# Differential attention heads written out in a fixed order of VectorE, ScalarE and GpSimd

## The chip, the cores and the metric

The kernel runs on one core of one Trainium2 chip. A core has a matrix engine (TensorE, "PE" in the profile; its weight loads are "PEld"), VectorE ("DVE"), ScalarE ("ACT"), GpSimd ("POOL") and SyncE ("SP"), which issues most of the loads. The engines run side by side, each works off its own list of instructions in order, and they wait for one another through semaphores. The metric is the device time of one execution in microseconds (us): the median over runs, before against after.

## The reference

One block of a streaming encoder over 512 tokens (T) of width 1024 (D), float32, one layer. It adds three terms to the residual stream x:

```python
h = rms_norm(x, attn_norm_g)
z = h @ w_in                                   # MLA latents | diff q | diff k | diff v
y_mla  = mla_group(...)                        # 8 heads, 64 wide
y_diff = diff_group(...)                       # 4 heads, 128 wide
x = x + concat([y_mla, y_diff]) @ w_out
x = x + conv_ffn(rms_norm(x, ffn_norm_g), ...) # 1024 -> 2816 -> 1024, causal conv, silu
x = x + sigmoid(rms_norm(x, ple_norm_g) @ w_ple_gate) * (p @ w_ple_proj)
```

The part that matters here is the differential group. Each of its 4 heads has two query and key halves (m = 0, 1; 64 wide), one value (128 wide), and a bias by relative position:

```python
logits = q[m] @ k[m].T * scale + bias          # masked block-causally
probs  = softmax(logits)
attn   = probs[0] - lam * probs[1]
o      = rms_norm(attn @ v, out_g) * (1 - lam_init)
```

## The kernel before

Everything is kept as tiles of 128 partitions. A float32 matrix product is made of three products of rounded halves: an operand is split into a high half (a cast to fp32r on ScalarE) and a low half (the rest, a subtraction on VectorE), and `mm3` (L152) issues high x high, high x low and low x high. So every operand that comes out of a transpose costs one ScalarE and one VectorE instruction before TensorE can use it (`split`, L180): TensorE takes the high half of an activation first and its low half one matmul later. Weights are loaded by SyncE into a ring of three buffers (`load_raw`, L138) and split in the same way, 128x1024 at a time (`load_w`, L143; ScalarE L148, VectorE L149).

The kernel goes through input projection, MLA heads (8 heads x 4 query tiles), differential heads (4 heads h x 4 query tiles t, list `dslots`, L709), the output projection, the feed-forward part, and the per-layer gate. TensorE's order is that of the program text throughout (`manual_schedule`, L98). VectorE, ScalarE and GpSimd follow the program text only inside regions; outside them a planner orders their instructions by its own estimate of readiness. Before the change, there is no region from the fifth step of the MLA heads to the end of the differential heads; the planner may move work forward there, and a few places are tied to an earlier instruction by `issue_after`. The feed-forward region begins at L847.

The differential loop (L767 to L782) has 16 steps i = 4h + t. In step i it issues the logits of step i + 2 (`diff_logits`, L662), some "fill" units of the output projection, the transposes of the probabilities of step i (`probs_T`, L533, with a copy out of PSUM on ScalarE, L541), and the product with the values of step i - 1 (`diff_pv`, L685). For each m, `diff_logits` issues three TensorE products, VectorE's sum with the bias that also gives the row maximum (L675), ScalarE's exponential with its row sum (L676); then VectorE combines both m (L680 to L682). Keys and queries of the next head are transposed and split in step t = 0 (`diff_T`, L654). After the last value product of a head, ScalarE squares the output and copies it out, VectorE reduces the squares, GpSimd raises to the power -0.5, and VectorE scales (L693 to L707). The scaled output is transposed and split in step t = 2 of the next head (`y_split`, L613).

A fill unit is six matmuls of 128x512: `wo_units` (L638) makes the output projection for a block b of 128 output columns; the first 16 units (kq = 0, two per block) use the MLA outputs, the last four (kq = 1) the outputs of differential heads 0 and 1. A finished block is added to the residual on VectorE (`add_x`, L630). `FILL_DIFF` (L63) says how many units each step takes. After the loop come products of what is still missing (`early`, L801), in which the output of head 2 is needed first and that of head 3 from the transposes at L805 on; then the feed-forward part's first weights.

PSUM has eight banks: "lg" 3 for logits, "tp" 2 for transposes, "acc" 2 for the output projection, "ob" 1 for the head's output. A transpose into "tp" waits until the bank's last reader is done.

Of the kernel before, what the change touches and what calls it, by code (L numbers as in the profile page):

```python
# [62 lines left out]
FILL_DIFF = ((2, 1, 1, 1), (1, 1, 2, 1), (1, 2, 2, 1), (1, 1, 2, 2))  # L63
# [26 lines left out]
def _f32(ap):  # L90
    return ap.bitcast(F32)
# [3 lines left out]
def hybrid_block(ctx: ExitStack, tc: tile.TileContext, a: dict, out: bass.AP):  # L95
# [537 lines left out]
    wo2 = {}  # L633

    def wo_w(kq, dq):
        return load_w(a["w_out"][kq, dq], 1024, f"o{kq}{dq}")

    def wo_units(kq, dqs, nk):  # L638

        for dq in dqs:  # L640
            w = wo_w(kq, dq)
            if kq:
                wo2[dq] = w
            for b in (2 * dq, 2 * dq + 1):
                ps = bank("acc", f"o{kq}{b}")
                for k in range(0, nk, 2):
                    mm3(ps, wo_blocks(4 * kq + k, 4 * kq + k + 2, b, w), k == 0, k == nk - 2)
                    if k == nk - 2:
                        add_x(b, ps)
                    yield  # L650
# [3 lines left out]
    def diff_T(h, c):  # L654
        ps = bank("tp" if h else "acc", f"d{c}T{h}")
# [3 lines left out]
        split(h_, l_, ps, dcol if c == 0 else None)  # L659
        df["qk", h, c] = (h_, l_)  # L660

    def diff_logits(h, t):  # L662
# [3 lines left out]
        s0 = df["s0", h][:, t:t + 1]  # L666
        (qh_, ql_), (kh_, kl_) = df["qk", h, 0], df["qk", h, 1]
        pms, s1 = [], sm.tile([P, 1], F32, tag="s1", bufs=4, name="s1")
        for m in range(2):
# [3 lines left out]
            pm = pm_tile("pmd")  # L673
            nm = sm.tile([P, 1], F32, tag="nm", bufs=4, name="nmd")
            V.tensor_tensor_reduce(out=pm[:, :n], in0=ps[:, :n], in1=strips[0][:, h, T - n:], scale=1.0, scalar=3e38, op0=ALU.add, op1=ALU.min, accum_out=nm)  # L675
            S.activation(pm[:, :n], pm[:, :n], AF.Exp, bias=nm, scale=-1.0, accum_out=s0 if m == 0 else s1)  # L676
            pms.append(pm)

        cf = sm.tile([P, 1], F32, tag="cf", bufs=4, name="cf")
        V.reciprocal(cf, s1)  # L680
        V.scalar_tensor_tensor(cf, cf, nlam, s0, op0=ALU.mult, op1=ALU.mult)
        V.scalar_tensor_tensor(pms[0][:, :n], pms[1][:, :n], cf, pms[0][:, :n], op0=ALU.mult, op1=ALU.add)  # L682
        df["pm", h, t] = pms[0]

    def diff_pv(h, t):  # L685
        if t == 0:
            df["po"] = bank("ob", f"do{h}")
        po, pt = df["po"], df.pop(("pt", h, t))
        for j in range(t + 1):
            TE.matmul(po[:, tsl[t]], pt[:, tsl[j]], zd[2][j][:, h * P:(h + 1) * P], start=j == 0, stop=j == t)  # L690
        if t < NT - 1:
            return
        s0 = df["s0", h]  # L693
        yn = tt(f"yd{h}")
        sq = sq_tile("sqo")[:, :T]
        S.activation(sq, po, AF.Square)
# [743 lines left out]
```

## Time and profile before

| | |
|---|---|
| median of 3 runs | 655.91 us (654.86 to 656.41) |
| profiled execution | 655.36 us, its span 653.5 us |
| TensorE busy | 642.6 us (98%) |
| VectorE busy | 475.3 us (73%) |
| ScalarE busy | 362.4 us (55%) |
| GpSimd busy | 57.0 us (9%) |
| mean granted TensorE clock | 0.995 |

The profile is of one execution; times in it count from the start of its span. A line of the order in time reads: start, duration, engine, line of the kernel, operation, output<-inputs, shape, count, and in brackets how long the engine stood idle before it and what it waited for. A line of the groups reads: line, engine, operation, names, shapes, count | busy us, mean ns of one | idle us before them. In the tables by stretch each engine's busy time is followed by its number of instructions; PEclk is the granted clock of TensorE as a share of full speed. Names: `dl` logits of the differential heads, `pmd` their probabilities, `pTd` and `pt` those transposed in PSUM and SBUF, `do` the head's output in PSUM, `yd` the same in SBUF, `yT` it transposed, `yh` and `yh5l` its halves (0 to 3 MLA, 4 to 7 differential heads 0 to 3), `o` the output projection, `hi_o`, `lo_o` its weights, `st` the halves of queries and keys.

### The profile page before, as it was taken

What the parts mean: (1) busy time and instruction counts of PE and PEld (TensorE: products, weight loads), DVE (VectorE), ACT (ScalarE), POOL (GpSimd) and SP (SyncE); (2) the same over time, 40 slices, a digit from 0 to 9 for tenths busy, and PEclk for the clock granted to TensorE, in tenths of its full rate; (3) what the DMA queues carried; (4) which work ended last, traced back from release to release, by engine and by line L of the source; (5) the groups of instructions that cost most, each with busy time, mean ns of one, the idle gap of its engine ahead of it and who ended that gap; (6) DMA issues with size and microseconds to landing.
All of it is one profiled execution on the core that took longest, in us unless ns stands there. A gap on an engine that the chain in (4) does not pass through costs nothing.

```text
span 653.5 us, 10266 instructions
## 1 busy us (share of the span) xinstructions
PE 642.6 (98%) x3932; PEld 569.8 (87%) x3932; DVE 475.3 (73%) x860; ACT 362.4 (55%) x631; POOL 57.0 (9%) x93
## 2 busy tenths in 40 slices
PE   9999999999998999999999999999999999999997
PEld 9988888888777787889999999999999999988886
DVE  6789587666877677888886767677767676759444
ACT  7787666457665445656554645554454545637211
POOL 1520040000000121000100000000001000000000
PEclk9999999999998999999999999999999999999999
DMA  8241224143110157536675646564646464542121
GB/s 308 89 162 46 84 82 161 66 135 123 33 34 2 64 178 241 150 93 172 173 207 136 182 114 178 119 190 128 179 112 178 114 177 113 178 129 62 35 80 49
DMA packets 29912, 82.63 MB, mean 126 GB/s; under 512 B 3100, under 2 KB 4124, under 8 KB 29736
## 3 DMA queue, kind: packets, MB, share of 16 engines
q1 hardware_dynamic: 23816, 69.17, 31.8%
q0 software_dynamic: 5616, 12.33, 10.8%
q8 instruction: 31, 0.51, 0.3%
q10 hardware_dynamic: 432, 0.49, 0.2%
q14 instruction: 17, 0.14, 0.1%
HBM read 77.77 MB, written 5.52 MB: 127 GB/s over the span
## 4 chain that ended last, share of the span: by engine, by line
PE 87%; DVE 6%; ACT 4%; DMA 1%; issue 1%; POOL 0%; ACTq 0%; POOLq 0%
PE dn L157 6%; PE dn L156 6%; PE dn L155 6%; PE gx L157 4%; PE gx L155 4%; PE gx L156 4%; PE g L155 4%; PE g L156 4%; PE g L157 4%; PE zd L155 3%; PE zd L157 3%; PE zd L156 3%; PE pg L155 2%; PE pg L157 2%; PE pg L156 2%; PE u L155 2%
## 5 line engine op out<-in xcount | busy, mean ns | idle before, releaser
L827 DVE TENSOR_TENSOR wSl<-rS,wSh 128x1024 fp32r<-128x1024 f32 x21 | 25.7, 1224 | 44.3 <-ACT wSh L823 44.2
L157 PE MATMUL dn<-ah,lo_dn 128*128 128x512 f32 x144 | 56.4, 392 | 0.0
L156 PE MATMUL dn<-al,hi_dn 128*128 128x512 f32 x144 | 56.3, 391 | 0.0
L155 PE MATMUL dn<-ah,hi_dn 128*128 128x512 f32 x144 | 56.0, 389 | 0.0
L944 POOL DMA_DIRECT2D rS<-in_w_gu x19 | 22.7, 1194 | 251.0 <-DVE cv L1111 138.9
L823 ACT CAST wSh<-rS 128x1024 fp32r<-128x1024 f32 x21 | 22.1, 1051 | 35.6 <-PE gy L156 35.3
L155 PE MATMUL zd<-hi_d,xh 128*128 128x512 f32 x96 | 39.3, 410 | 0.0
L156 PE MATMUL zd<-lo_d,xh 128*128 128x512 f32 x96 | 37.6, 391 | 0.0
L631 DVE TENSOR_TENSOR x<-x,dn 128x512 f32<-128x512 f32 x44 | 29.9, 679 | 6.3 <-PE dn L157 6.1
L827 DVE TENSOR_TENSOR wTl<-rA,wTh 128x1024 fp32r<-128x1024 f32 x19 | 23.3, 1225 | 14.0 <-ACT wTh L823 13.4
L573 ACT ACTIVATE pm<-ml,nm,rq 128x128 f32<-128x128 f32 (+3 forms) x32 | 19.7, 617 | 22.6 <-DVE nm L571 22.6
L157 PEld LDWEIGHTS dn<-ah,lo_dn 128*128 128x128 f32 x144 | 27.0, 188 | 5.7
L156 PEld LDWEIGHTS dn<-al,hi_dn 128*128 128x128 f32 x144 | 27.0, 188 | 5.3
L155 PEld LDWEIGHTS dn<-ah,hi_dn 128*128 128x128 f32 x144 | 27.1, 188 | 5.2
L155 PE MATMUL o<-yh,hi_o 128*128 128x512 f32 x64 | 27.7, 432 | 1.0 <-DVE x L631 1.0
L676 ACT ACTIVATE pmd<-pmd,nmd 128x128 f32<-128x128 f32 (+3 forms) x32 | 17.9, 559 | 17.7 <-DVE nmd L675 17.7
L823 ACT CAST wAh<-rA 128x1024 fp32r<-128x1024 f32 x21 | 22.0, 1050 | 9.7 <-DMA rA<-in_w_gu 9.4
L1114 ACT ACTIVATE cv<-cv 128x512 f32<-128x512 f32 x22 | 13.9, 631 | 23.9 <-DVE cv L1111 23.8
L570 DVE TENSOR_REDUCE nm<-ml 128x1 f32<-128x128 f32 (+3 forms) x32 | 15.6, 487 | 15.1 <-PE ml L157 15.1
L155 PE MATMUL g<-b2h,wAh 128*128 128x256 f32 (+1 forms) x88 | 26.4, 300 | 0.2 <-ACT g L1067 0.2
L156 PE MATMUL g<-b2l,wAh 128*128 128x256 f32 (+1 forms) x88 | 26.2, 297 | 0.0
L157 PE MATMUL g<-b2h,wAl 128*128 128x256 f32 (+1 forms) x88 | 26.2, 297 | 0.0
(467 smaller groups left out, 2226.8 us busy)
## 6 DMA issues: line engine op xcount, KB each, us to landing
rA<-in_w_gu SPq DMA_DIRECT2D x22, 512.0 KB, 3.8
rS<-in_w_gu SPq DMA_DIRECT2D x22, 512.0 KB, 3.6
rS<-in_w_gu POOLq DMA_DIRECT2D x19, 512.0 KB, 6.0
raw_dn<-in_w_down SPq DMA_DIRECT2D x18, 512.0 KB, 5.9
raw_d<-in_w_d SPq DMA_DIRECT2D x12, 512.0 KB, 3.7
r<-in_w_gu SPq DMA_DIRECT2D x19, 256.0 KB, 6.1
raw_o<-in_w_out SPq DMA_DIRECT2D x8, 512.0 KB, 3.7
rS_pg<-in_w_pg SPq DMA_DIRECT2D x6, 512.0 KB, 4.0
```

Of the source, the lines that this page charges most:

```text
L155: TE.matmul(ps, xh, wh, start=first and i == 0, stop=False, skip_group_check=again)
L156: TE.matmul(ps, xh, wl, start=False, stop=False, skip_group_check=again)
L157: TE.matmul(ps, xl, wh, start=False, stop=last and i == n - 1, skip_group_check=again)
L570: V.reduce_max(nm, ps[:, :n], axis=AX.X, negate=True)
L573: S.activation(pm[:, :n], ps[:, :n], AF.Exp, bias=nm, scale=r, accum_out=mla["ssum", h // 2][:, t, h % 2:h % 2 + 1])
L631: V.tensor_tensor(xb(b), xb(b), ps, op=ALU.add)
L676: S.activation(pm[:, :n], pm[:, :n], AF.Exp, bias=nm, scale=-1.0, accum_out=s0 if m == 0 else s1)
L823: S.copy(h_, src)
L827: V.tensor_tensor(l_, src, _f32(h_), op=ALU.subtract)
L944: nc.gpsimd.dma_start(sums[f].rearrange("p (i c) -> p i c", i=2), a["w_gu"][f][:, :2048].rearrange("p (i c) -> p i c", i=2)[:, :, :512], a ...
L1114: S.activation(cv, cv, AF.Silu)
```

## The change

VectorE, ScalarE and GpSimd follow the program text from the first differential logits on, through to the feed-forward region. The text is written out for that:

- Maximum, exponential and combination of a step are separate calls. In step i: the logits of step i + 2 on TensorE; then maximum and exponential of its m = 0, the combination of step i + 1, the maximum of m = 1, the high halves of what was transposed at the end of step i - 1 (`pend`), the exponential of m = 1, their low halves; the low half of a weight (`WO_LO`); fill units; transposes; value product; the high half of the next weight (`WO_HI`).
- Transposes are spread: queries of head h + 1 at the end of step t = 0, keys of head h + 2 at t = 2, the output of head h - 1 at t = 3. Their splits come in the step that follows.
- The squares are summed by ScalarE, per step, 128x128 at a time with an accumulated sum, instead of one 128x512 square and a VectorE reduction.
- The scaling of heads 0 to 2 is on GpSimd, in step t = 1 of the next head. That of head 3 stays on VectorE.
- The output projection's weights are split at fixed steps: the first in the last MLA head, six in the loop, the last low half after it. The fill units are spread anew. The splits of the per-layer inputs (`pk`) come after the loop in fixed order.

```diff
-FILL_DIFF = ((2, 1, 1, 1), (1, 1, 2, 1), (1, 2, 2, 1), (1, 1, 2, 2))
+FILL_DIFF = ((1, 2, 1, 1), (1, 2, 1, 1), (1, 2, 1, 1), (1, 1, 1, 1))
...
+    def split_hi(h_, l_, src, col):
+        if col is None:
+            S.copy(h_, src)
+        else:
+            S.activation(h_, src, AF.Identity, scale=col)
+
+    def split_lo(h_, l_, src, col):
+        if col is None:
+            V.tensor_tensor(l_, src, _f32(h_), op=ALU.subtract)
+        else:
+            V.scalar_tensor_tensor(l_, src, col, _f32(h_), op0=ALU.mult, op1=ALU.subtract)
+
+    def y_T(i, src, col, tag="tp"):
+        ps = bank(tag, f"yT{i}")
+        for t in range(NT):
+            TE.transpose(ps[:, tsl[t]], src[:, tsl[t]], ident)
+        yh[i], yl[i] = th_tile(f"yh{i}")
+        return yh[i], yl[i], ps, col
...
     def diff_pv(h, t):
...
-        S.activation(sq, po, AF.Square)
-        df["copy"] = S.copy(yn, po)
-        V.reduce_sum(sso, sq.rearrange("p (t d) -> p t d", d=P), axis=AX.X)
+        S.activation(sq_tile("sqo")[:, :P], po[:, tsl[t]], AF.Square, accum_out=df["sso", h][:, t:t + 1])
+        if t == NT - 1:
+            df["y", h] = tt(f"yd{h}")
+            S.copy(df["y", h], po)
+
+    def diff_norm(h, eng):
...
         G.tensor_tensor(ro, mo, mhalf[:, :NT], op=ALU.pow)
-        df["scale"] = V.tensor_tensor(yv, yv, ro.unsqueeze(2).broadcast_to([P, NT, P]), op=ALU.mult)
+        return lambda: eng.tensor_tensor(yv, yv, ro.unsqueeze(2).broadcast_to([P, NT, P]), op=ALU.mult)
...
-    diff_logits(0, 0)
+    wo[0, 0] = wo_first[0]
+    region = tc.manual_schedule(engines={mybir.EngineType.DVE, mybir.EngineType.Activation, mybir.EngineType.Pool})
+    region.__enter__()
+    diff_mm(0, 0)
...
+    pend = [y_T(3, ymn[3], None)]
+    for x in pend:
+        split(*x)
+    pend = [diff_T(1, 1)]
+    WO_HI = {0: (0, 1), 3: (0, 2), 6: (0, 3), 9: (1, 0), 11: (1, 1), 13: (1, 2), 15: (1, 3)}
+    WO_LO = {1: (0, 1), 4: (0, 2), 8: (0, 3), 10: (1, 0), 12: (1, 1), 14: (1, 2)}
     for i, (h, t) in enumerate(dslots):
-        if i + 2 < len(dslots):
-            diff_logits(*dslots[i + 2])
-        if h + 1 < DH and t == 0:
-            diff_T(h + 1, 1)
+        new = dslots[i + 2] if i + 2 < len(dslots) else None
+        if new:
+            diff_mm(*new)
+            diff_max(*new, 0)
+            diff_exp(*new, 0)
+        if i + 1 < len(dslots):
+            diff_sum(*dslots[i + 1])
+        if new:
+            diff_max(*new, 1)
+        for x in pend:
+            split_hi(*x)
+        if new:
+            diff_exp(*new, 1)
+        for x in pend:
+            split_lo(*x)
+        if h and t == 1:
+            scale = diff_norm(h - 1, G)
+        if i in WO_LO:
+            wo_lo(*WO_LO[i])
         pump(FILL_DIFF[h][t])
         df["pt", h, t] = probs_T(df.pop(("pm", h, t)), t, f"d{h}{t}", True)
         if i:
             diff_pv(*dslots[i - 1])
-        if h + 1 < DH and t == 0:
-            diff_T(h + 1, 0)
-        if h and t == 2:
-            y_split(4 + h - 1, df["y", h - 1], ocol, "tp")
+        if i in WO_HI:
+            wo_hi(*WO_HI[i])
+        if h and t == 1:
+            scale()
+        pend = []
+        if t == 0 and h + 1 < DH:
+            pend.append(diff_T(h + 1, 0))
+        if t == 2 and h + 2 < DH:
+            pend.append(diff_T(h + 2, 1))
         if h and t == 3:
+            pend.append(y_T(4 + h - 1, df["y", h - 1], ocol))
             if h == 2:
                 fill.append(wo_units(1, range(2), 2))
-    pump()
+    for x in pend:
+        split(*x)
     diff_pv(*dslots[-1])
+    scale = diff_norm(DH - 1, V)
+    wo_lo(1, 3)
     pump(100)
...
+    pk, pkr = kvp.tile([P, 4, 1024], F32R, tag="kv", name="pk"), []
...
+    scale()
+    for i in range(2):
+        V.tensor_tensor(pk[:, 2 * i + 1], pkr[i], _f32(pk[:, 2 * i]), op=ALU.subtract)
```

More of the change, by code (lines that the diff above doesn't have):

```diff
@@ L652, in hybrid_block, with diff_T @@
     df = {}
-    def diff_T(h, c):
-        ps = bank("tp" if h else "acc", f"d{c}T{h}")
+    def diff_T(h, c, tag="tp"):
+        ps = bank(tag, f"d{c}T{h}")
         for t in range(NT):
@@ L658, in diff_T, with diff_mm @@
         h_, l_ = st[4 * (h % 2) + 2 * c], st[4 * (h % 2) + 2 * c + 1]
-        split(h_, l_, ps, dcol if c == 0 else None)
         df["qk", h, c] = (h_, l_)
-    def diff_logits(h, t):
+        return h_, l_, ps, dcol if c == 0 else None
+    def split_hi(h_, l_, src, col):
[14 more added lines that the diff above has]
+        return yh[i], yl[i], ps, col
+    def diff_mm(h, t):
         n = (t + 1) * P
@@ L672, in diff_logits, with diff_max, diff_exp, diff_sum @@
             mm3(ps[:, :n], [(qh_[r, tsl[t]], ql_[r, tsl[t]], kh_[r, :n], kl_[r, :n])])
[L673 to L677, printed above, removed]
+            df["ps", h, t, m] = ps
+    def diff_max(h, t, m):
+        n = (t + 1) * P
+        pm = pm_tile("pmd")
+        nm = sm.tile([P, 1], F32, tag="nm", bufs=4, name="nmd")
+        V.tensor_tensor_reduce(out=pm[:, :n], in0=df.pop(("ps", h, t, m))[:, :n], in1=strips[0][:, h, T - n:], scale=1.0, scalar=3e38, op0=ALU.add, op1=ALU.min, accum_out=nm)
+        df["pm", h, t, m] = pm, nm
+    def diff_exp(h, t, m):
+        n = (t + 1) * P
+        pm, nm = df["pm", h, t, m]
+        if m:
+            df["s1", h, t] = sm.tile([P, 1], F32, tag="s1", bufs=4, name="s1")
+        S.activation(pm[:, :n], pm[:, :n], AF.Exp, bias=nm, scale=-1.0, accum_out=df["s1", h, t] if m else df["s0", h][:, t:t + 1])
+    def diff_sum(h, t):
+        n = (t + 1) * P
+        pm = [df.pop(("pm", h, t, m))[0] for m in range(2)]
         cf = sm.tile([P, 1], F32, tag="cf", bufs=4, name="cf")
[L680 to L683, printed above, removed]
+        V.reciprocal(cf, df.pop(("s1", h, t)))
+        V.scalar_tensor_tensor(cf, cf, nlam, df["s0", h][:, t:t + 1], op0=ALU.mult, op1=ALU.mult)
+        V.scalar_tensor_tensor(pm[0][:, :n], pm[1][:, :n], cf, pm[0][:, :n], op0=ALU.mult, op1=ALU.add)
+        df["pm", h, t] = pm[0]
     def diff_pv(h, t):
@@ L687, in diff_pv @@
             df["po"] = bank("ob", f"do{h}")
+            df["sso", h] = sm.tile([P, NT], F32, tag="sso", name="sso")
         po, pt = df["po"], df.pop(("pt", h, t))
@@ L804, in hybrid_block @@
         if n == 5:
-            y_split(7, df["y", 3], ocol, "tp")
+            split(*y_T(7, df["y", 3], ocol))
         early[b] = bank("acc" if n < 2 else "lg" if n < 5 else "tp", f"o3{b}")
@@ L831, in hl @@
         return lo_(*hi_(*x, **k))
[L833 to L840 removed]
     gu = lambda f, c0, c1: a["w_gu"][f][:, 512 * c0:512 * c1]
     rpp = raw_w(a["w_pp"][1], "rS", "pp1", bufs=3)
[L844 to L848 removed]
+    wpp.append(hl(rpp, "wT", "pp1"))
+    wA0 = hi_(raw_w(gu(0, 0, 2), "rA", 0, bufs=2), "wA", 0, bufs=2)
+    W = {0: {0: wA0[:2]}}
     nr_ = [ffn.tile([P, 1024], F32, tag="raw", bufs=2, name=f"nr{i}") for i in range(2)]
```

72 lines of the change are left out of this document (29 added, 43 removed).

## The prediction

> **What bounds the kernel now.** I read the page first, then the busy time by stretch, then TensorE in order of time where the differential heads run (first logits at 160.6 us, last transposed head output at 231.9 us), then ScalarE and VectorE around each of its gaps.
>
> ```profile
> span 653.5 us, 10266 instructions
> PE 642.6 (98%) x3932; PEld 569.8 (87%) x3932; DVE 475.3 (73%) x860; ACT 362.4 (55%) x631; POOL 57.0 (9%) x93
> PE 87%; DVE 6%; ACT 4%; DMA 1%; issue 1%; POOL 0%; ACTq 0%; POOLq 0%
> ```
>
> TensorE is the bound, and none of its instructions goes away: all transposes, products and fill units stay. So the change can only win or lose the time in which TensorE stands or runs slowly.
>
> ```profile
> core 0: us, PE busy (x) PEld busy (x) DVE busy (x) ACT busy (x) POOL busy (x), PEclk, DMA share, GB/s
> 164.00:226.00 62.00, 59.20 (x362) 46.88 (x361) 48.39 (x140) 37.41 (x97) 3.05 (x3) 0.97 0.09 29
> ...
> 200.00:205.00 5.00, 5.00 (x19) 3.64 (x16) 4.12 (x9) 1.59 (x4) 1.01 (x1) 0.66 0.00 0
> ...
> 201.00:202.00 1.00, 1.00 (x3) 0.75 (x3) 1.00 (x3) 0.00 (x0) 0.38 (x1) 0.50 0.00 0
> ```
>
> ```profile
> 157.27 0.66 PE L617 MATMUL yT<-ident,ym 128*128 128x128 f32 x4 [0.45 <-DVE st L184]
> ...
> 199.07 0.66 PE L657 MATMUL d0T<-ident,zd 128*128 128x128 f32 x4 [1.69 <-ACT pt L541]
> ...
> 220.64 0.50 PE L155 MATMUL o<-yh,hi_o 128*128 128x512 f32 x1 [0.96 <-DVE x L631]
> ```
>
> ```profile
> PEld do L690 <- ACT pt L541: 0.3, 1, 0.3
> ```
>
> In the heads TensorE loses four pieces: 1.69 us at 197.4 to 199.1; then (1 - 0.66) x 5 = 1.7 us, because the granted clock falls to 0.50 right behind that gap; 0.96 us at 220.6; and 0.3 us at the products behind the last step but one. That is 4.65 us. A fifth, 0.45 us, lies just ahead at 157.3. Two of the causes:
>
> ```profile
> 197.81 1.04 ACT L148 CAST hi_o<-raw_o 128x1024 fp32r<-128x1024 f32 x1
> 198.76 0.26 ACT L541 COPY pt<-pTd 128x128 f32<-128x128 f32 x1
> ```
>
> ```profile
> 155.33 1.22 DVE L149 TENSOR_TENSOR lo_o<-raw_o,hi_o 128x1024 fp32r<-128x1024 f32 x1
> ...
> 156.53 0.69 DVE L184 TENSOR_TENSOR st<-d1T,st 128x512 fp32r<-128x512 f32 x1
> ```
>
> The 1.69 us gap is a transpose (the query transpose of the next head) that needs the bank which this short copy frees, while ScalarE was still at a cast of output weights that the planner put in front. The 0.45 us gap is a split behind the other half of such a weight.
>
> **The change part by part.** Its durations:
>
> ```profile
> L676 ACT ACTIVATION_READ_ACCUMULATOR pmd<-pmd,nmd 128x1 f32 x32 | 6.0, 187 | 0.0
> ...
> L675 DVE CUSTOM_DVE_ANT_0 pmd<-dl,strip 128x512 f32<-128x512 f32 x8 | 5.3, 685 | 0.0
> ...
> L149 DVE TENSOR_TENSOR lo_o<-raw_o,hi_o 128x1024 fp32r<-128x1024 f32 x3 | 3.7, 1220 | 0.0
> ...
> L676 ACT ACTIVATE pmd<-pmd,nmd 128x128 f32<-128x128 f32 x8 | 3.2, 400 | 5.5 <-DVE nmd L675 5.5
> ...
> L148 ACT CAST hi_o<-raw_o 128x1024 fp32r<-128x1024 f32 x3 | 3.1, 1042 | 0.0
> ...
> L706 DVE TENSOR_TENSOR yd<-yd,ro 128x512 f32<-128x512 f32 x4 | 2.8, 692 | 2.7 <-POOL ro L704 2.7
> L699 DVE TENSOR_REDUCE sso<-sqo 128x4 f32<-128x512 f32 x4 | 2.7, 680 | 1.6 <-ACT sqo L696 1.6
> ...
> L696 ACT ACTIVATE sqo<-do 128x512 f32<-128x512 f32 x4 | 2.4, 593 | 1.4 <-PE do L690 1.2
> ...
> L187 DVE SCALAR_TENSOR_TENSOR st<-d0T,dcol,st 128x512 fp32r<-128x512 f32 x3 | 2.2, 746 | 0.5 <-ACT st L186 0.5
> ...
> L186 ACT ACTIVATE yh<-yT,ocol 128x512 fp32r<-128x512 f32 x3 | 2.1, 688 | 0.8 <-PE yT L617 0.8
> ```
>
> *Load of the engines.* VectorE had 48.39 us between 164 and 226. Three reductions (0.68) and three scalings (0.69) leave this stretch, which is 4.1 us; but where three weights were made there, six are now, 3 x 1.22 = 3.7 us more, because the planner no longer puts them under the MLA heads. So about 48 us remain. ScalarE had 37.4 us; 15 squares with a sum come at, by the 128x128 exponential, 0.40 + 0.19 each (8.9 us; 0.26 us by the copy of that size from below, 3.9 us), four casts (4.2 us), and three squares of 128x512 (1.8 us) and two casts of the per-layer inputs (2.1 us) go: 41.6 to 46.6 us. Both stay under TensorE's 57 to 60 us, so the load alone costs nothing; with the cover gone it would cost what the third rival says.
>
> *Order.* In each step the short copy of the probabilities now stands in front of the cast of weights, and the transposes that a split needs are issued a step earlier. The tightest place is steps 4h + 1 and 4h + 2, where the next head's first logits need the split of its query. TensorE gets there after the last logits (0.9 us by the widths around them), two units of six matmuls at 0.23 (2.8; row 213.74 below) and about 0.6 of transposes and products: 4.3. VectorE, from about 0.9, has two maxima (0.69 each), a sum of about 1.1 and the low half of the split (0.75): 4.1. Behind it in step 1 the weight's low half (1.22) ends at 5.3, when step 2's unit asks for it (4.3 + 0.5 + 0.5). That fits, and everywhere else there is a step or more to spare: the sum that a transpose needs is made one step ahead, the residual add one and a half. So all four pieces go: -4.65 us, with 0.3 us to the worse where the two ends meet. For the 0.45 us piece, four of the five weights made under the MLA heads leave, among them the one at 155.3; the bounds are -0.45 and +1.2 (the first weight, now asked for in the last MLA head, lands there instead); I take -0.45, since the row names the cause.
>
> *New waits.* Two transposed outputs are used at once. The output of head 1 is transposed at the end of step 11 and used by the fill unit of step 12, whose split stands behind that step's first exponential on ScalarE and behind both maxima and a sum on VectorE. The old step with the same logits gives the times:
>
> ```profile
> 211.98 0.45 PE L155 MATMUL dl<-st 64*128 64x384 f32 x2
> ...
> 212.71 0.50 PE L155 MATMUL o<-yh,hi_o 128*128 128x512 f32 x1
> ...
> 213.51 0.39 PE L155 MATMUL o<-yh,hi_o 128*128 128x512 f32 x1
> 213.74 0.40 PE L156 MATMUL o<-yh5l,hi_o 128*128 128x512 f32 x1
> ```
>
> ```profile
> 212.80 0.56 DVE L675 CUSTOM_DVE_ANT_0 pmd<-dl,strip 128x384 f32<-128x384 f32 x1 [0.55 <-PE dl L157]
> ...
> 213.28 0.16 DVE L680 RECIPROCAL cf<-s 128x1 f32<-128x1 f32 x1
> ...
> 213.74 0.48 DVE L682 SCALAR_TENSOR_TENSOR pmd<-pmd,cf 128x256 f32<-128x256 f32 x1
> ```
>
> ```profile
> 213.40 0.62 ACT L676 ACTIVATE pmd<-pmd,nmd 128x384 f32<-128x384 f32 x1 [0.48 <-DVE nmd L675]
> ```
>
> Counted from the logits' start, TensorE wants the high half of this output at 213.51 - 211.98 = 1.53. The exponential begins at 1.42 and takes 0.62, the split's high half 0.69: ready at 2.73, a wait of 1.2 us. VectorE: maximum from 0.82 to 1.38, sum 213.28 to 214.22 = 0.94, second maximum 0.56, low half 0.75: ready at 3.63. TensorE gets there at 2.73 + 0.23 and waits 0.67. Together 1.9 us.
>
> The output of head 2 is transposed in step 15, only one set of products ahead of its use:
>
> ```profile
> 181.12 1.06 PE L690 MATMUL do<-zd,pt 128*128 128x128 f32 x8
> ```
>
> From the end of the transpose TensorE has 1.06 us of this. ScalarE still has a square (0.59, begun 0.44 earlier, so 0.15), the last weight's cast (1.04) and then the split (0.69): 1.88, a wait of 0.8 us; the low half follows 0.75 later, TensorE 0.23 later: 0.5 more. Together 1.3 us. Bounds for both: nothing, if each split is ready in time, and 1.9 + 1.3 + 1.2 (one weight's work more in front).
>
> *The end of the stage.* The last weight's low half, the scaling on VectorE and the low halves of the per-layer inputs, 1.22 + 0.69 + 2 x 1.22 = 4.4 us, now lie between the last product and the transpose of head 3's output. 27 matmuls at 0.23 = 6.2 us stand there on TensorE: hidden, 0. The loads of those inputs now wait for weight buffers freed in steps 12 and 14, several us ahead of their casts: 0.
>
> *GpSimd's scaling*, 128x512, is not in the trace; the nearest rows:
>
> ```profile
> L880 POOL TENSOR_TENSOR nr<-nr,nsq x3: 1292/1297/1620, 238.5 to 241.3; 128x512 f32<-128x512 f32 x3
> ```
>
> ```profile
> L882 DVE TENSOR_TENSOR nr<-nr,nsq x2: 692/756/821, 240.9 to 243.1; 128x512 f32<-128x512 f32 x2
> ```
>
> 1.3 to 1.6 us, issued two steps (over 5 us) ahead of the transpose that reads it: 0 on TensorE's path, from below too. VectorE's row beside it lengthened by 0.13 us, which I take as the price on VectorE.
>
> *Sum*: -4.65 - 0.45 + 1.9 + 1.3 = -1.9 us. The profiled execution took 655.36 us (span 653.5): 653.5 us after. The median of the runs, 655.91, lies 0.55 us above it, so I forecast 654.0.
>
> **The rivals.** (1) *The clock falls behind a new wait.* For it: 1.69 us of standing was followed by half the clock at a cost of 1.7 us, and step 12 stands 1.9 us. Against it: that wait is in two pieces with a matmul between, and the 0.96 us gap was followed by nothing. Time: 654.0 + 1.7 = 655.7, no change. [...]
>
> (2) *TensorE waits nowhere.* If both splits are in time: 654.0 - 3.2 = 650.8. Against it stands the walk above; for it only that the trace of before has no such wait.
>
> (3) *Slower: VectorE sets the pace.* Each step's list on VectorE begins with a maximum that waits for logits, so it may stand 0.82 us (row above) in each, 3.3 us a head.
>
> ```profile
> 178.39 0.45 PE L155 MATMUL dl<-st 64*128 64x384 f32 x2
> ...
> 193.60 0.45 PE L155 MATMUL dl<-st 64*128 64x384 f32 x2
> ```
>
> TensorE takes 193.60 - 178.39 = 15.2 us a head, and 62 / 15.2 = 4.1 heads lie in the stretch, so VectorE has 48 / 4.1 = 11.7 us of work a head. With the standing that is 15.0: it fits by 0.2. From the point where GpSimd's scaling adds more than that to VectorE, the head is VectorE's. At a full 1.3 us each head loses 1.1 us, three heads 3.3 us, and one fall of the clock 1.7: 654.0 + 5.0 = 659.0. Against it: where VectorE is late it does not stand, so work and standing don't add fully. [...] The 0.13 us above speaks for less.
>
> **How the numbers follow.** Forecast 0.45 (653 to 655), rival 1 0.27, rival 2 0.11, rival 3 0.17. About 0.2%, 1.3 us, is what a measurement of this kernel can tell from no change. Below 654.6: rival 2 and 0.39 of the forecast, 0.50. Above 657.2: nearly all of rival 3, 0.16. Between: 0.34. The range leaves out about half of rival 2 and most of rival 3: 650.8 to 657.6; it also holds the bounds of the new waits and of the 0.45 us piece (654.0 + 1.2 + 1.65 = 656.9).
>
> **What would show it.** In TensorE's order of time the waits at the query transpose of head 3, at the residual add in head 3 and at the last products should be gone; instead there should be one of about 1.9 us in two pieces in the fourth head's first fill unit, released by the splits of the second head's output, and one of about 1.3 us at the first early product after the last head. The clock row there tells rival 1. If TensorE waits for sums or residual adds in several steps, it is rival 3. The forecast is wrong if the stretch from the first logits to the last transposed output (71.3 us) doesn't shorten by 1 to 2 us, or if the time is lost outside it.

## The result, and the profile after

| | before | changed |
|---|---|---|
| median (lowest to highest) | 655.28 us of 14 runs (653.98 to 657.53) | 659.55 us of 14 runs (657.29 to 662.23) |
| ratio to before | | 1.0067 (95% interval 1.0050 to 1.0085) |
| profiled execution, its span | 655.36 us, 653.5 us | 661.3 us, 659.5 us |

The changed kernel is slower by 4.3 us, and the forecast of 654.0 us missed in size and in sign. Of the 6.0 us between the two profiled spans, 2.4 us were lost in the first 30 us, where the code is the same (mean granted clock 0.94 there, 1.00 before): that belongs to this execution. Before the heads 0.5 us was won, as forecast (the gap at the transposes of the MLA output is down from 0.45 to 0.19 us, and one of 0.24 behind it is gone). The rest is in the differential heads. TensorE of the changed kernel in order of time, first and last row of that stage:

```profile
162.55 0.34 PE L155 MATMUL dl<-st 64*128 64x128 f32 x2
...
237.92 0.60 PE L683 MATMUL yT<-ident,yd 128*128 128x128 f32 x4
```

From the first logits to the last transposed output that is 75.4 us, against 71.3 before: 4.1 us more, where 1 to 2 us less were forecast. Names beyond the list above: `sqo` the squares, `cf` the factor of the combination, `nmd` the row maximum, `x` the residual, `raw_o` a weight as loaded, `ident` the identity that transposes. The same view, all waits of that stretch that show a bracket:

```profile
170.95 0.63 PE L663 MATMUL d0T<-ident,zd 128*128 128x128 f32 x4 [1.36 <-DVE st L676]
...
197.90 0.30 PE L683 MATMUL yT<-ident,yd 128*128 128x128 f32 x1 [0.80 <-DVE st L676]
...
202.22 0.63 PE L663 MATMUL d0T<-ident,zd 128*128 128x128 f32 x4 [0.37 <-DVE yh4l L678]
...
216.81 0.50 PE L155 MATMUL o<-yh,hi_o 128*128 128x512 f32 x1 [1.51 <-ACT yh L672]
...
217.59 0.80 PE L156 MATMUL o<-yh5l,hi_o 128*128 128x512 f32 x1 [0.28 <-DVE yh5l L678]
...
225.84 0.71 PE L729 MATMUL do<-zd,pt 128*128 128x128 f32 x4 [0.31 <-ACT sqo L730]
...
231.10 0.50 PE L155 MATMUL o<-yh,hi_o 128*128 128x512 f32 x1 [0.37 <-ACT yh L186]
231.89 0.50 PE L156 MATMUL o<-yh6l,hi_o 128*128 128x512 f32 x1 [0.28 <-DVE yh6l L187]
```

The waits of before are gone as to their causes. In their place stand three at transposes into a "tp" bank (steps 0, 7 and 8; 2.5 us in brackets), which I had not forecast (that of step 8, 0.37 us, is at the very query transpose of head 3 that waited 1.69 us before); the forecast wait for the output of head 1 in step 12 (1.8 us); a small one at a value product, for the square of the step before in the one "ob" bank; and the forecast wait for the output of head 2 behind the loop (0.65 us). Behind the largest the granted clock falls. By stretches of one microsecond, same columns as in the prediction:

```profile
164.00:226.00 62.00, 57.37 (x341) 44.29 (x341) 48.61 (x139) 38.80 (x121) 5.29 (x6) 0.97 0.15 43
217.00:218.00 1.00, 0.72 (x2) 0.41 (x2) 1.00 (x2) 0.38 (x2) 0.00 (x0) 0.77 0.00 0
218.00:219.00 1.00, 1.00 (x4) 0.70 (x4) 0.82 (x2) 0.00 (x0) 0.00 (x0) 0.50 0.00 0
219.00:220.00 1.00, 1.00 (x7) 1.00 (x6) 0.54 (x1) 0.27 (x1) 0.00 (x0) 0.50 0.37 33
220.00:221.00 1.00, 1.00 (x6) 0.78 (x7) 0.00 (x0) 0.23 (x2) 0.00 (x0) 0.52 0.59 221
```

0.23 + 0.50 + 0.50 + 0.48 = 1.7 us of TensorE's time go there. The brackets add up to 5.3 us, with the clock 7.0, against 4.65 before: 2.3 of the 4.1 us. A wait can cost more than its bracket. In step 12 the last product ahead of the wait is this:

```profile
214.91 0.39 PE L157 MATMUL o<-yh,lo_o 128*128 128x512 f32 x1
```

From its start to 216.81 are 1.90 us where 0.23 is the pace, so 1.67 were lost against a bracket of 1.51. There are eight waits now, against two with a bracket and one of 0.3 us at a weight load before. If each of the five more costs 0.16 us beyond its bracket, as this one does, that is an estimated 0.8 us; about 1 us stays unaccounted for.

VectorE had 48.61 us of work in 62 us, so it was not full, as forecast. Its waits in that stretch (what waited, for what, us in total, times, longest), changed kernel:

```profile
DVE pmd L703 <- PE dl L157: 7.4, 7, 2.3
```

It stands 7.4 us for logits with work behind them in its list that could have been done: in six of these waits, 6.7 us together, the exponentials that the next combination needs were done before the wait or within 0.2 us of its start. Step 0 shows what such a list does, though VectorE's wait there is for ScalarE and not for logits. VectorE of the changed kernel in order of time:

```profile
167.47 0.69 DVE L184 TENSOR_TENSOR yh3l<-yT,yh 128x512 fp32r<-128x512 f32 x1 [1.20 <-ACT yh L183]
168.08 0.55 DVE L703 CUSTOM_DVE_ANT_0 pmd<-dl,strip 128x384 f32<-128x384 f32 x1
...
169.00 0.48 DVE L720 SCALAR_TENSOR_TENSOR pmd<-pmd,cf 128x256 f32<-128x256 f32 x1
169.63 0.56 DVE L703 CUSTOM_DVE_ANT_0 pmd<-dl,strip 128x384 f32<-128x384 f32 x1
...
170.12 0.69 DVE L676 TENSOR_TENSOR st<-d1T,st 128x512 fp32r<-128x512 f32 x1
```

First it stands 1.20 us for a high half from ScalarE, then come a maximum, the combination of step 1, a second maximum, and only then the low half of the keys, whose end frees the bank for the queries' transpose at 170.95: it begins 2.0 us behind the first maximum. The last exponential that the combination needs was done, with its row sum, at 166.97, so about half of the combination (0.5 of 0.93 us) could have been made in the 1.20 us. ScalarE, same view:

```profile
166.37 0.51 ACT L711 ACTIVATE pmd<-pmd,nmd 128x256 f32<-128x256 f32 x1 [0.45 <-DVE nmd L703]
166.78 0.19 ACT L711 ACTIVATION_READ_ACCUMULATOR pmd<-pmd,nmd 128x1 f32 x1
```

### The profile page after: what moved, and what is told of

It reads as the page before. It is cut to its first block, busy times and chain, and to the rows that moved or that the text cites. A ratio compares the mean times of both kernels' runs of the same rounds, so it can differ in the third digit from the quotient of the medians.

```text
span 659.5 us, 10290 instructions
## 1 busy us (share of the span) xinstructions
PE 645.9 (98%) x3932; PEld 571.4 (87%) x3932; DVE 474.4 (72%) x853; ACT 364.8 (55%) x659; POOL 62.3 (9%) x96
## 4 chain that ended last, share of the span: by engine, by line
PE 80%; DVE 11%; ACT 6%; DMA 2%; issue 1%; ACTq 0%; DVEq 0%; SPq 0%
PE dn L156 6%; PE dn L157 6%; PE dn L155 6%; PE gx L157 4%; PE gx L155 4%; PE gx L156 4%; PE g L155 3%; PE g L156 3%; PE g L157 3%; PE zd L155 3%; PE zd L157 3%; PE zd L156 3%; PE pg L155 2%; PE pg L157 2%; PE pg L156 2%; PE mo L583 2%
## 5 line engine op out<-in xcount | busy, mean ns | idle before, releaser
L906 DVE TENSOR_TENSOR wAl<-rA,wAh 128x1024 fp32r<-128x1024 f32 x22 | 26.8, 1218 | 1.8 <-ACT wAh L902 1.8
```

The lines of the kernel that those rows point to most:

```text
L906: V.tensor_tensor(l_, src, _f32(h_), op=ALU.subtract)
```

## The experiments

Each kernel was compared with the kernel before on the same chip. That came to 654.4 to 655.6 us from one group of runs to the next, so the ratios are compared. No kernel leaves any of the computation out. "Planner" means that the fixed order begins after the 16 steps. There is no kernel 7.

| kernel | median us | ratio to before (95%) |
|---|---|---|
| changed kernel | 659.55 | 1.0067 (1.0050 to 1.0085) |
| 1 splits first in all steps | 662.47 | 1.0103 (1.0083 to 1.0124) |
| 2 fill unit of step 12 in step 13 | 658.10 | 1.0042 (1.0027 to 1.0057) |
| 3 splits first in steps 0, 7, 8 | 659.55 | 1.0067 (1.0052 to 1.0082) |
| 4 scaling on VectorE | 660.64 | 1.0080 (1.0060 to 1.0100) |
| 5 planner | 653.35 | 0.9977 (0.9960 to 0.9993) |
| 6 planner, VectorE's list fixed | 658.51 | 1.0053 (1.0037 to 1.0069) |
| 8 squares whole | 659.75 | 1.0079 (1.0058 to 1.0099) |
| 9 another fixed order | 654.58 | 0.9997 (0.9984 to 1.0010) |
| 10 combination moved | 658.75 | 1.0062 (1.0044 to 1.0080) |
| 11 planner, fill unit in step 13 | 653.13 | 0.9966 (0.9953 to 0.9978) |
| 12 as 9, fill unit in step 13, keys early | 653.80 | 0.9975 (0.9960 to 0.9990) |
| 13 as 5, scaling on VectorE | 657.48 | 1.0038 (1.0021 to 1.0055) |
| 14 as 10, keys early | 656.00 | 1.0019 (1.0007 to 1.0032) |
| 15 high halves first | 658.76 | 1.0049 (1.0031 to 1.0068) |
| 16 as 11, scaling on VectorE | 655.87 | 1.0008 (0.9990 to 1.0025) |
| 17 as 5, transposes not spread | 654.29 | 0.9985 (0.9974 to 0.9996) |
| 18 as 11, squares whole | 654.27 | 0.9981 (0.9967 to 0.9995) |
| 19 as 16, squares whole | 656.38 | 1.0018 (1.0007 to 1.0030) |

**Are the waits themselves the cause?** The first theory took each wait for a fault of its own, to be mended where it stands.

Kernel 1:

```diff
             diff_mm(*new)
+        for x in pend:
+            split(*x)
+        if new:
             diff_max(*new, 0)
...
-        for x in pend:
-            split_hi(*x)
...
-        for x in pend:
-            split_lo(*x)
```

> The changed kernel with one edit: in every step of the differential loop both halves of what was transposed in the step before (pend) are split first, ahead of maximum, exponential and combination. Bank theory (TensorE loses 2.8 us at the two "tp" banks in steps 0, 7 and 8, because the low half that frees a bank stands in VectorE's fixed list behind two maxima and a combination; 1.53 + 0.87 + 0.39 us between starts in the changed kernel's trace): these three waits go, and the wait for the output of head 1 in step 12 gets shorter by one exponential (0.5 to 0.8 of 2.2 us) and may lose the clock's fall behind it (about 1.7 us): 2.8 to 5.3 us below the changed kernel, 654 to 657 us. Rival (VectorE as a whole is late, since GpSimd's scaling and the fixed list take its time): the waits only move to maxima or combinations that are now behind the splits: within 1 us of the changed kernel.

Kernel 2: the last row of `FILL_DIFF` is (0, 2, 1, 1) instead of (1, 1, 1, 1).

> The changed kernel with one edit: step 12 takes no fill unit and step 13 two, so that nothing in step 12 needs the output of head 1. If the wait there (1.51 + 0.28 us idle, 2.17 us between starts) is the cause of the clock's fall behind it (217.4 to 220.8 at 0.50, worth 1.7 us), both go: 3.9 us below the changed kernel. If the wait alone goes and the clock falls anyway: 2.2 us below. If the wait is taken over by the next thing in the chain (the transposes of step 12, the value product of step 11): under 1 us. The waits at the "tp" banks in steps 0, 7 and 8 stay as they are by every theory.

Kernel 3: as kernel 1, but `if i in (0, 7, 8)`; the order stays in the other steps.

> The changed kernel with one edit: the splits come first in steps 0, 7 and 8 alone, the steps that wait at a "tp" bank. Bank theory: 2.8 us below the changed kernel, the wait of step 12 and the clock's fall stay. If the bank waits are only a sign of a late VectorE: under 1 us, with new waits in steps 1, 8 and 9. The difference to the kernel with the splits first in all steps gives what the order is worth in step 12.

Kernel 4: `diff_norm(h - 1, V)` instead of `diff_norm(h - 1, G)`.

> The changed kernel with one edit: the scaling of heads 0 to 2 is on VectorE instead of GpSimd. Lock theory (GpSimd's 1.0 to 1.5 us of scaling shuts VectorE out, whose combination beside it took 1.62 and 1.57 us against 0.75 alone, and this makes the splits late): each scaling gives VectorE back 0.8 us and takes 0.75 us: no net change on VectorE, so under 0.5 us either way in time, with the combinations back at 0.75 us. Rival (GpSimd is late, and the output of head 1 for step 12 with it): 1 us or more below the changed kernel. Third (VectorE is the bound): 0.5 to 1 us above.

The theory fell. Splits first made it slower by 0.36% (the intervals just touch), in three steps alone it changed nothing, and the fill unit moved gave 1.6 us by the ratios instead of 2.2 to 3.9 (the intervals overlap). In kernel 3 the bank waits came down from 2.5 to 0.31 us, but 0.72 us for the low half of a weight and 0.33 us for a split of the queries came. TensorE of kernel 1, its waits up to step 12:

```profile
175.75 0.80 PE L157 MATMUL o<-yh,lo_o 128*128 128x512 f32 x1 [1.53 <-DVE lo_o L302]
...
198.38 0.63 PE L683 MATMUL yT<-ident,yd 128*128 128x128 f32 x4 [0.83 <-DVE st L184]
...
205.36 0.50 PE L157 MATMUL o<-yh,lo_o 128*128 128x512 f32 x1 [0.72 <-DVE lo_o L302]
...
218.40 0.50 PE L155 MATMUL o<-yh,hi_o 128*128 128x512 f32 x1 [1.57 <-ACT yh L186]
```

The bank wait of step 0 went, and 1.53 us for the low half of a weight came, in the next step but one; now VectorE stood at the head of its list for the high half on ScalarE (1.87 us in step 1). In kernel 2 nothing needs head 1's output early, and this came in its place:

```profile
219.87 0.50 PE L155 MATMUL o<-yh,hi_o 128*128 128x512 f32 x1 [1.94 <-DVE x L631]
```

Two blocks are finished in step 13 now, and their sums into x, which free the "acc" banks, stand last in VectorE's list. The clock fell behind it as well (0.50 from 221 to 224 us). So whatever stands last is late. Kernel 4 can't be told from the changed kernel (the intervals overlap widely). By itself that leaves GpSimd's scaling open, since by the expectation VectorE pays about as much for the scaling as it gets back; kernel 5 below, which keeps the scaling on GpSimd and is fast, shows that the scaling as such isn't the cause. What VectorE loses where the two meet (last section) is part of what the order decides: 2.2 us in the changed kernel (1.62 and 1.57 us where 0.75 is usual, and 1.73 where 1.22 is), while no combination of kernel 5 took more than 0.75 us; between these two lie 5.9 us.

**Is it the fixed list?** Kernels 5 and 6, and 9 with another list; 8 puts another part of the change back, the squares.

Kernel 5 (kernel 6 has `tc.manual_schedule(engines={mybir.EngineType.DVE})` around the steps):

```diff
-    region = tc.manual_schedule(engines={mybir.EngineType.DVE, mybir.EngineType.Activation, mybir.EngineType.Pool})
-    region.__enter__()
     diff_mm(0, 0)
...
+            with tc.issue_after(df["max"].ins):
                 wo_lo(*WO_LO[i])
...
+            with tc.issue_after(df["max"].ins):
                 wo_hi(*WO_HI[i])
...
+    region = tc.manual_schedule(engines={mybir.EngineType.DVE, mybir.EngineType.Activation, mybir.EngineType.Pool})
+    region.__enter__()
     for x in pend:
         split(*x)
     diff_pv(*dslots[-1])
```

> The changed kernel with the fixed order taken away from the 16 steps: the region begins after the loop, and in it the planner orders VectorE, ScalarE and GpSimd; the weights' halves are tied to a maximum of their step, so that they are not moved into the MLA heads. All other parts of the change stay (spread transposes, squares per step, scaling on GpSimd, fill units). List theory: each instruction of VectorE's fixed list waits for the one ahead of it, which waits for a cast or for logits, and TensorE waits wherever it needs something from the end of the list soon; putting the splits first only moved the waits (1.53 us for lo_o, 0.72 us for lo_o, 1.57 us for the output of head 1 stayed). Then the planner's order gives 4 to 5.5 us back: 654 to 655.5 us. Rival (the other parts cost the time: transposes in consecutive steps on two "tp" banks, squares per step on the one "ob" bank, scaling on GpSimd): 657 us or more. If the order costs half of it: 655.5 to 657 us.

> As the kernel with the planner's order in the loop, but VectorE alone keeps the fixed list there; ScalarE and GpSimd are ordered by the planner. If VectorE's list is what is late: within 1.5 us of the changed kernel, 658 to 660.5 us. If ScalarE's list is (the cast of a weight, 1.05 us, ahead of the high halves that VectorE then waits for: 1.87 us in the kernel with the splits first): the time of the kernel with the planner's order, 657 us or less.

Kernel 8: in `diff_pv` the square of `po` is taken once, at `t == NT - 1`, with `V.reduce_sum` behind it.

> The changed kernel with the squares as before: one 128x512 square per head on ScalarE and a reduction on VectorE, all else as changed. Bank theory of the value products (each waits for the square of the step before, since both use the one "ob" bank: 0.31 us and about 0.24 us idle in the changed kernel): 0.3 to 0.7 us below the changed kernel. Against it stands 0.6 us of reduction per head in VectorE's list, in step 4, 8 and 12, of which the splits of these steps would be late: up to 1 us above. Likeliest: within 0.7 us.

Kernel 9 (with `diff_sum(0, 1)` ahead of the loop as well):

```diff
         if new:
             diff_mm(*new)
-            diff_max(*new, 0)
-            diff_exp(*new, 0)
-        if i + 1 < len(dslots):
-            diff_sum(*dslots[i + 1])
-        if new:
-            diff_max(*new, 1)
         for x in pend:
             split_hi(*x)
         if new:
-            diff_exp(*new, 1)
+            for m in range(2):
+                diff_max(*new, m)
+                diff_exp(*new, m)
         for x in pend:
             split_lo(*x)
...
         pump(FILL_DIFF[h][t])
+        if new:
+            diff_sum(*new)
```

> The changed kernel, all three engines in a fixed order, with another order: in step i the high halves of what was transposed come first on ScalarE; VectorE takes both maxima of step i + 2, then the low halves, the low half of the weight, the sum into x, and at the end of the step the combination of step i + 2, where the changed kernel puts the combination of step i + 1 between the two maxima. List theory: the order alone decides, and one in which nothing waits for an exponential of its own step until the end gives most of it back: 2.5 to 5 us below the changed kernel, 654.5 to 657 us. Rival (any fixed order costs the same, since VectorE then waits for the exponentials, 4.7 us in seven waits in the kernel before, with all else behind them): within 1 us of the changed kernel.

It is the order. Without this one the other parts of the change give 0.2% (1.5 us by the ratio); with it they lose 0.7%: 0.9%, 5.9 us, lie between them. And a fixed order as such need not cost that: kernel 9 has one, differs from the changed kernel in nothing else, and is 0.7% (4.6 us) faster; it can't be told from the kernel before. With the squares whole (kernel 8) the wait at the value product is gone from the trace, and the time can't be told from the changed kernel's.

Kernel 6 does not show which engine's list is at fault. Its time is the one expected if VectorE's list is (658 to 660.5 us), but the waits are others: 0.36 us in step 0, none in steps 7 and 8, and most of the loss in step 12. ScalarE and then TensorE of kernel 6 in order of time:

```profile
212.78 1.04 ACT L298 CAST hi_o<-raw_o 128x1024 fp32r<-128x1024 f32 x1 [2.10 <-DMA raw_o<-in_w_out]
213.73 0.68 ACT L672 ACTIVATE yh<-yT,ocol 128x512 fp32r<-128x512 f32 x1
```

```profile
214.46 0.80 PE L155 MATMUL o<-yh,hi_o 128*128 128x512 f32 x1 [3.18 <-ACT yh L672]
```

The planner put the cast of a weight, which waits 2.10 us for its load, ahead of the high half of head 1's output, and the clock stands at 0.66 from 214 to 219 us, 1.7 us more. So the expected time came out there by another wait.

Waits of VectorE from 164 to 226 us in kernel 5:

```profile
DVE cf L718 <- ACT pmd L711: 4.6, 7, 1.5
DVE pmd L703 <- PE dl L157: 2.2, 4, 0.9
```

It waits for the exponentials of its own step now, and little for logits: the combination is made at once, in time that the changed kernel stands idle. Step 0 of kernel 5, VectorE and then TensorE in order of time:

```profile
165.82 0.48 DVE L720 SCALAR_TENSOR_TENSOR pmd<-pmd,cf 128x256 f32<-128x256 f32 x1
166.32 0.69 DVE L184 TENSOR_TENSOR yh3l<-yT,yh 128x512 fp32r<-128x512 f32 x1
166.93 0.55 DVE L703 CUSTOM_DVE_ANT_0 pmd<-dl,strip 128x384 f32<-128x384 f32 x1
...
167.40 0.55 DVE L703 CUSTOM_DVE_ANT_0 pmd<-dl,strip 128x384 f32<-128x384 f32 x1
...
167.88 0.69 DVE L676 TENSOR_TENSOR st<-d1T,st 128x512 fp32r<-128x512 f32 x1
```

```profile
168.71 0.63 PE L663 MATMUL d0T<-ident,zd 128*128 128x128 f32 x4 [0.19 <-DVE st L676]
...
211.72 0.50 PE L155 MATMUL o<-yh,hi_o 128*128 128x512 f32 x1 [0.36 <-ACT yh L672]
212.50 0.50 PE L156 MATMUL o<-yh5l,hi_o 128*128 128x512 f32 x1 [0.29 <-DVE yh5l L678]
```

The combination of step 1 stands ahead of both, the two maxima stand together, the low half of the keys begins 0.95 us behind the first, and the three rows of TensorE are all its waits in the heads: 0.84 us, where the changed kernel has 5.3.

**Which move in the list?** Kernel 10 takes `diff_sum(*dslots[i + 1])` from between the maxima and puts `diff_sum(*new)` at the end of the step (and so `diff_sum(0, 1)` ahead of the loop); nothing else. Kernel 15 puts `split_hi` ahead of `diff_exp(*new, 0)` and nothing else. Kernel 14 is kernel 10 with `split(*diff_T(1, 1))` ahead of the loop.

> The changed kernel with one edit to its fixed order: the combination of step i + 2 stands at the end of step i, behind the sum into x, instead of between the two maxima of step i + 1. ScalarE's order stays. If the place of the combination alone is what makes the splits, lo_o and the sum into x late (1.0 us in front of them, while VectorE stands idle 7.4 us in seven waits for logits ahead of it): 4 to 5.5 us below the changed kernel, 654 to 656 us, as with the whole other order (654.6). If it takes the high halves first on ScalarE as well: 656 to 659 us.

> The changed kernel with one edit: ScalarE makes the high halves of what was transposed first in each step, ahead of both exponentials; VectorE's list stays as it is. If ScalarE's order matters by itself: 2 to 4 us below the changed kernel. If VectorE's list is what is late (with ScalarE ordered by the planner and VectorE's list fixed, the kernel came out 3.5 us above the kernel before): within 1.5 us of the changed kernel.

> The kernel with the combination at its own step's end as the only move, and with the keys of head 1 split before the loop. That kernel's time (3.1 us above the kernel before) holds a wait of 2.04 us in step 0 and 1.7 us of halved clock behind it. If the place of the combination is the main fault of the changed kernel's list, both go and it comes to 3.7 us less: 0.5 us or less above the kernel before (about 655 us). If the order on ScalarE is needed too: 1.5 to 3 us above the kernel before.

Kernel 10 missed its expectation: 0.3 us by the ratios. In its trace the bank waits of steps 7 and 8 are gone and the wait of step 12 is down from 1.51 to 1.08 us, but one wait grew:

```profile
169.20 0.63 PE L663 MATMUL d0T<-ident,zd 128*128 128x128 f32 x4 [2.04 <-DVE st L676]
```

with the clock at 0.83 over the ten microseconds behind. With the keys split earlier (kernel 14) 2.8 us came back, a little under the 3.7 worked out, and it stands 3.1 us below the changed kernel. The high halves alone are worth 1.2 us by the ratios (the intervals overlap). So no single move does it. Kernel 14 has two, the combination and the keys; the keys alone weren't run, so the share of each is open. Kernel 14 still waits 1.07 and 0.28 us for head 1's output, behind the first exponential on ScalarE; in kernel 9, whose order puts the high half ahead of it, these are 0.18 and 0.28 us.

**What are the other parts worth, and what is the fastest?** With the order out of the way: kernels 11 and 12 move the fill unit (and the keys), 13 and 16 put the scaling on VectorE, 17 puts the transposes back to where they were before the change, 18 and 19 the squares.

> The kernel with the planner's order in the loop, and step 12 without a fill unit, step 13 with two. Its only waits of TensorE over 0.2 us are 0.36 and 0.29 us for the output of head 1 in step 12: if they go and nothing takes their place, 0.6 us below it, 652.7 us. If the sum into x is late then, as in the changed kernel with this fill (1.94 us): 653.5 to 655 us.

> The fixed order with the combination at the end of its own step, and two more edits: step 13 takes step 12's fill unit, and the keys of head 1 are split before the loop and not behind two maxima of step 0. This takes away its waits of 1.15 us (bank in step 0) and 0.18 + 0.28 us (output of head 1): 1.6 us below it, 653.0 us, if they don't move; 654 to 655 us if the sum into x or lo_o is late in their place.

> The kernel with the planner's order in the loop, with the scaling of heads 0 to 2 on VectorE. GpSimd's scaling costs VectorE 0.8 us each time where the two meet, VectorE's own costs it 0.75 us: within 0.5 us of the kernel with the planner's order (653.35 us) if VectorE has slack; 0.5 to 1.5 us slower if the scaling on VectorE makes splits or the output of a head late.

> The planner's order, no fill unit in step 12, and the scaling on VectorE. If the scaling on VectorE cost 4 us only through the wait for the output of head 1 in step 12 (1.88 us and 1.7 us of halved clock), it is within 0.7 us of the same kernel with the scaling on GpSimd (2.2 us below the kernel before). If VectorE's load is the reason: 1.5 to 4 us slower than that.

> The planner's order in the loop, with the transposes where they were before the change (keys and queries of the next head in step t = 0, the output in t = 2, each split at once); squares, scaling and fill units as changed. If the spread is what the forecast's gain came from: the waits of the kernel before come back (1.69 us for the queries' bank and 1.7 us of halved clock), and it is 2.5 to 3.5 us slower than with the transposes spread, 656 us or more. If the spread is worth nothing: within 0.7 us of it, 653 to 654 us.

> The fastest version so far (planner's order, no fill unit in step 12) with the squares as before: one 128x512 square per head and a reduction on VectorE. Its one wait of TensorE over 0.2 us in the loop past step 0 is 0.35 us at a value product, for the square of the step before. Bank theory: it goes, 0.35 us less. Rival: the reduction (0.6 us of VectorE per head, and a wait for the square ahead of it) makes the scaled output or a split late: up to 2 us more.

> The same with the scaling on VectorE. If the scaling on VectorE cost its 2.7 us through the load (scaling delays lo_o, lo_o frees the buffer of the next load, the cast waits for that load, the square waits behind the cast, the value product waits 1.84 us for the square), then with no square there the wait goes: 1.8 us or more below the version with the scaling on VectorE and squares per step, near 653.5 us. If VectorE's load is the reason: no better than that version (0.1 per cent above the kernel before).

Kernel 11 has the lowest ratio, 0.34% (2.2 us) under the kernel before; its interval overlaps those of kernels 5 and 12. Kernel 12, with its fixed order, comes close to it; there 0.62 us for a sum into x took the place of the waits removed. Kernel 13 stands 1.88 us for head 1's output in step 12, with the clock at 0.66 from 210 to 220 us; without that unit (kernel 16) more than half of its loss against kernel 11 remains. Between 11 and 16 lie 2.75 us by the ratios for the scaling's engine; the intervals are apart. Kernel 16 shows a wait with a long chain, ScalarE and TensorE in order of time:

```profile
210.10 1.04 ACT L298 CAST hi_o<-raw_o 128x1024 fp32r<-128x1024 f32 x1 [1.23 <-DMA raw_o<-in_w_out]
211.05 0.27 ACT L730 ACTIVATE sqo<-do 128x128 f32<-128x128 f32 x1
...
211.46 0.71 PE L729 MATMUL do<-zd,pt 128*128 128x128 f32 x4 [1.84 <-ACT sqo L730]
```

A weight's load is late, because the low half that frees its buffer was (it ended at 206.2 us and the load was issued at 206.27; 204.7 and 204.74 in kernel 11, where the cast waits 0.46 us); the cast waits for the load, the square behind the cast, and the value product for the square's bank. I took that chain for the price of the scaling. Kernel 19 has no square there, and is no faster than 16: the wait came back elsewhere.

```profile
222.72 0.63 PE L538 MATMUL pTd<-ident,pmd 128*128 128x128 f32 x4 [1.63 <-DVE pmd L720]
```

Kernel 19 also pays for the reduction on VectorE, so the fairer pair is 18 and 19, which both lack that square and differ in the scaling's engine alone: 0.37%, 2.4 us, about as much as 11 and 16. So that chain isn't the price; that the wait turned up elsewhere is what the other theory, VectorE's load, expected, but no run tests that theory by itself. Squares on ScalarE save 1.0 us by 11 and 18, spread transposes 0.5 us by 5 and 17: in both pairs the intervals overlap, so neither is told from nothing.

## Why the prediction was wrong, point by point

- *Load of the engines* was about right. From 164 to 226 us the changed kernel has 48.61 us on VectorE (about 48 said) and 38.80 on ScalarE (41.6 to 46.6 said), but it is late and that window holds 341 of TensorE's matmuls where 362 stood before; in kernel 5, with the same work and 373 matmuls in the window, it is 50.16 and 42.10.
- *Order* is the step that failed: "That fits, and everywhere else there is a step or more to spare". The walk asked when the logits of the next head need their split. It didn't ask for the bank: a transpose in the same step (0, 7, 8) waits until that split has read the bank of the last one (1.36, 0.80 and 0.37 us), and there are two banks with one taken by the probabilities in every step. So the same low half is wanted a step earlier than the walk had it. The walk also added up VectorE's instructions back to back from the logits on; the trace shows it standing first, 7.4 us in seven waits. What the runs showed in place of "that fits" is 4.1 us more in the heads. The bank by itself isn't the whole of it, since mending it in steps 0, 7 and 8 alone gave nothing (kernel 3): it is the order of the whole list, 4.6 us against another fixed one (kernel 9) and 5.9 us against the planner's (kernel 5). Which place in the list costs how much stays open.
- *All four pieces go* was right by the rows but for the 0.37 us at the query transpose of head 3, and worth nothing, since others came. The 1.7 us of clock among them was not lost in every execution (see below). The 0.45 us at the end of the MLA heads went but for 0.19.
- *New waits*: 1.9 us said for the output of head 1, 1.8 in brackets (2.1 by starts); 1.3 said for that of head 2, 0.65 in brackets. The mechanism was right in both, the second term too large; in the first the cast of a weight (214.53 to 215.57) stood ahead of ScalarE's exponential too.
- *The clock* (rival 1) fell behind the first of them in the profiled execution, for 1.7 us as said.
- *GpSimd's scaling* took 1.04 us twice and 1.54 once (1.3 to 1.6 said), and the 0.13 us for VectorE was wrong where it mattered (0.87 and 0.82 us on a combination, 0.51 on a low half): see below. Yet it isn't why the kernel is slower (kernel 5).
- *Rival 3* said 659.0 us, and 659.55 was measured, but not by its mechanism: VectorE is late without being full, and kernel 5, with the same instructions on VectorE and GpSimd in another order, is fast. No run shows the full 1.3 us of VectorE for each scaling in its sum: the three scalings of the changed kernel cost VectorE 2.2 us together. That the time came out was luck.
- *The sum*, 653.5 to 654.0, is what the other parts give without the list (653.35 us), for other reasons than mine: I credited the gain to the fixed order and the spread; in the runs only the scaling that left VectorE is surely worth something. So that nearness is luck too.

## What to carry to other kernels

In a fixed order, don't ask whether an engine has time for its list, but what stands behind each instruction that waits, and put work that is ready ahead of it: here the order alone cost 4.6 to 5.9 us while VectorE was 22% idle. When each mended wait turns up elsewhere at the same size (1.36 us gone and 1.53 come in kernel 1, 1.51 and 0.28 gone and 1.94 come in kernel 2), the waits aren't the fault; test the order as a whole before its places. And list for each transpose the bank it takes and who frees it, as well as who reads it.

## What the runs showed of the hardware

Beside GpSimd's scaling some instructions of VectorE took longer and others didn't. Changed kernel, GpSimd and VectorE in order of time:

```profile
191.87 1.04 POOL L743 TENSOR_TENSOR yd<-yd,ro 128x512 f32<-128x512 f32 x1
...
191.83 1.62 DVE L720 SCALAR_TENSOR_TENSOR pmd<-pmd,cf 128x512 f32<-128x512 f32 x1
```

Kernel 11, same views:

```profile
184.36 1.04 POOL L743 TENSOR_TENSOR yd<-yd,ro 128x512 f32<-128x512 f32 x1
...
184.22 0.75 DVE L678 SCALAR_TENSOR_TENSOR st<-d0T,dcol,st 128x512 fp32r<-128x512 f32 x1
184.88 0.68 DVE L703 CUSTOM_DVE_ANT_0 pmd<-dl,strip 128x512 f32<-128x512 f32 x1
```

The combination, with two inputs in SBUF, took 1.62 us beside this scaling and 1.57 beside the next (0.75 in the kernel with the scaling on VectorE). With the third, which took 1.54 us itself instead of 1.04, it took 0.75, and the low half of a weight behind it, also with two inputs in SBUF, 1.73 instead of 1.22. A low half and a maximum, which read one input from PSUM, took 0.75 and 0.68 us in kernel 11, as in the kernel before (0.75 and 0.69), and all that its three scalings met there were such instructions, of 0.68 to 0.75 us. Whether the place of the inputs makes the difference wasn't tried by itself, nor whether this is part of why the scaling on GpSimd is worth 2.75 us in kernel 11 and nothing sure in the changed kernel.

The clock fell behind waits that were shorter than the fall itself (0.50 from 217.5 to 220.9 us in the changed kernel, 3.4 us), and not by their length alone: behind 1.51 and 0.28 us (changed kernel), 1.53 (kernel 1), 1.94 (kernel 2), 2.04 (kernel 10), but also behind 0.93 and 0.55 (kernel 15); not behind 1.36 (changed kernel, step 0), 1.63 (kernel 19) or 1.84 (kernel 16), where the clock stood at 1.00 from 170 to 176, 220 to 230 and 210 to 220 us. From 23 to 26 us of the changed kernel it was 0.50 too, with no wait from 18 us on but one of 0.26. Each fall cost about 1.7 us; in kernel 13, with 0.66 over ten microseconds, it was 3.4.

Nor does it fall in every execution of one kernel. Of the 23 executions of the kernel before that were run beside kernels 18 and 19, nine had a mean granted clock of 0.998 or more and took 654.0 to 655.0 us; fourteen had 0.996 or 0.997 and took 655.2 to 658.2. Of the changed kernel's 14, three had 0.999 and took 657.3 to 657.7 us; eleven had 0.993 to 0.997 and took 658.6 to 662.2. So some 3 us of its loss are there at the full clock, and the rest goes with a lower one. Of the thirteen waits of TensorE of 1.5 us or more between 160 and 240 us in these traces eleven had a fall behind them. So in this kernel such a wait should be counted with a chance of 1.7 us on top, and a trace of one execution doesn't tell how large that chance is.
